# Mean and root of four RMS norms as wide tiles instead of per-token columns, in a float32 encoder trunk

## The chip, the cores and the metric

The kernel runs on one core of one Trainium2 chip. The metric is the device time of one execution, in microseconds (us). The kernel before takes 2190.19 us, the median of three runs (2189.79 to 2191.43).

## The reference

One encoder layer and a final norm, for two groups of tokens that share their weights: a prompt of 1024 tokens and a sample of 256. The change touches two of the RMS norms: `h = rmsnorm(x, norm_ffn_w)` ahead of the feed-forward block, and the last norm of the prompt.

```
def rmsnorm(x, w):
    y = x * lax.rsqrt(jnp.mean(x * x, -1, keepdims=True) + EPS)
    return y * w
...
def encoder_layer(...):
    ...                                  # token mixing, then cross-attention, each x = x + ...
    h = rmsnorm(x, norm_ffn_w)
    gu = h @ ffn_w_gate_up
    x = x + (silu(gu[..., :D_FF]) * gu[..., D_FF:]) @ ffn_w_down
    return x
...
trunk: return rmsnorm(x, final_norm_w)   # prompt and sample
```

## The kernel before, in words

Activations lie feature-major: 1024 features are eight tiles of 128 partitions (k or m = 0 to 7), and the tokens run along the free axis in three blocks: block 0 (prompt, 512 tokens), block 1 (prompt, 512) and block 2 (sample, 256). In the text they are also x0, x1 and x2, after the residual tiles that hold them.

A product in float32 accuracy is made of three products in the type float32r: each operand is split in a rounded part "hi" and a rest "lo" (`split`, L124 to L126: ScalarE copies hi, VectorE or GpSimd subtracts to get lo), and hi·hi, hi·lo and lo·hi are added up in a PSUM bank (`mm3`, L110, which calls `mm`, L108). So nearly every TensorE row of the profile is L108, and nearly every split L125 and L126.

A norm needs, for each token, a sum over 1024 features, which lie on partitions and tiles. `Norm.add` (L241) squares a tile on ScalarE (L250, L253) and adds it to `nacc`, a tile of 128 partitions by tokens (L254, on VectorE, in the last norm on GpSimd). `Norm.rest` (L257) then does:

- the sum: for each 128 tokens a true float32 product of `nacc` with a column of ones. TensorE makes each float32 product in two passes, so four of them are eight instructions. The result is one column for each 128 tokens;
- the root, on VectorE (L271 and `rsqrt`, L225): a first guess from the bits and three Newton steps, eleven instructions on 128x4 numbers;
- after a lag, the spreading of the root over all partitions: four float32 products of the root's columns (`nst`, broadcast) with the identity, eight instructions again;
- the normalisation, L289: x times weight times the spread root, which stands in a PSUM bank. In the last norm some tiles (`SHARED`) go another way: ScalarE multiplies by the weight, and GpSimd by a copy of the root (L281, L284, L285).

The order of work. TensorE's order is the program's own: the main generator issues matmuls and advances a modelled clock (`K.clock`), and side generators (the norms) are pumped when that clock passes their due time. `yield lag` in a norm thus sets after how many modelled nanoseconds its sum, and with `lag2` its spreading, is put among the main matmuls. TensorE works in that order strictly; where a matmul's input is late, all that follows waits. The other engines' orders are made by a scheduler from a cost model, and each engine also works strictly in its order.

Around the feed-forward norm: `OutProj.run` (L1451) makes the attention's output projection, first two tiles m of all blocks, then m = 2 to 7 of block 0, then of block 1, then of block 2. Each tile's evacuation (L1462) adds to x and then to the norm. After a block's last tile its x is stored to memory (`x2d`, L1492) and its norm is started as a side (L1497). The normalisation overwrites x in place, so it waits for that store. Meanwhile GpSimd and ScalarE prepare feed-forward weights (`after`, L1835: two weight splits, then four additions at L1847). Then `ff_first` (L2052) multiplies four products of the normalised blocks 0 and 1 for the first feed-forward tile: `pa` and `pu` of block 0, `pb` and `pv` of block 1, then the sample. Block 2's sum stands half way in `pa`, its spreading in `pb`. The results go through a SiLU (tanh on ScalarE, L1914). The feed-forward products are made with sums and differences of the normalised halves, which VectorE prepares from x0 and x1 (`make_r1`, L1867; `make_r2`, L1874 and L1875; `make_t34`, L1882).

At the end: `down_prompt` (L2203) finishes block 1 of the prompt and then block 0, each followed by `last_norm` (L2260) as a side, beside the last prompt products and the sample's products. Normalised tiles are stored by transfers that ScalarE's and SyncE's queues issue in turn (L2264).

Of the kernel before, what the change touches and what calls it, by code (L numbers as in the profile page):

```python
# [17 lines left out]
P = 128  # L18
D = 1024
KT = D // P  # L20
# [6 lines left out]
EPS = 1e-6  # L27
# [10 lines left out]
S_MIX, S_XA, S_MEM, S_FFN, S_FIN, S_CONV, S_DNW, S_LNW, S_LNB = 0, 8, 16, 24, 32, 40, 100, 101, 105  # L38
# [16 lines left out]
class Trunk:  # L55
# [68 lines left out]
    def split(self, hi, lo, src, eng=None):  # L124
        self.last_hi = self.nc.scalar.activation(hi, src, AF.Copy).ins  # L125
        (eng or self.nc.vector).tensor_tensor(out=lo, in0=src, in1=f32(hi), op=ALU.subtract)  # L126
# [37 lines left out]
def trunk_kernel(ctx: ExitStack, tc: tile.TileContext, a):  # L164
    nc = tc.nc
    V, S, G, T, SY = nc.vector, nc.scalar, nc.gpsimd, nc.tensor, nc.sync
    K = Trunk(ctx, tc, a)
# [19 lines left out]
    n = 0  # L187
# [44 lines left out]
    class Norm:  # L232
# [21 lines left out]
                (eng or V).tensor_tensor(out=self.acc, in0=self.acc, in1=sq, op=ALU.add)  # L254
            self.k += 1

        def rest(self, xk, wcol, sink, pace=1300, shared=(), lag=1500, ks=range(KT), inplace=False, ready=None, halves=1, lag2=2800, rooms=()):  # L257

            p, n = self.p, self.n
            nb = n // P  # L260
            yield lag
# [7 lines left out]
            y = p.tile([P, 4 if p is xp else 16], F32, tag="nst", name="nst", bufs=2)[:, :nb]  # L269
# [12 lines left out]
            for k in ks:  # L282
                if k in shared:
                    S.activation(xk(k), xk(k), AF.Copy, scale=sm[:, wcol + k : wcol + k + 1])  # L284
                    G.tensor_tensor(out=xk(k), in0=xk(k), in1=rb, op=ALU.mult)  # L285
                    sink(k, xk(k))
                    continue
                t = bank() if k in rooms else xk(k) if shared or inplace else p.tile([P, 512], F32, tag="nsq", name="nt", bufs=self.sq)[:, :n]
                V.scalar_tensor_tensor(out=t, in0=xk(k), scalar=sm[:, wcol + k : wcol + k + 1], in1=pb[:, :n], op0=ALU.mult, op1=ALU.mult)  # L289
                sink(k, t)  # L290
                yield pace * n / 512

    def rstd_of(nm, y, lag, lag2=0, halves=1):
        n = nm.n
# [109 lines left out]
    parts = []  # L404
# [7 lines left out]
    pb = bank()  # L412
# [1016 lines left out]
    class OutProj:  # L1429
# [21 lines left out]
        def run(self, xsrc, scale, wcol, xpool, store, sinks=None, then=None, after=None):  # L1451


            ps = (xpool,) * 3 if sinks is None else (x0p, xhp, xpool)
            x = [p.tile([P, KT, n], F32, tag=f"x{b}", name=f"x{b}") for b, (p, (_, n)) in enumerate(zip(ps, BLOCKS))]
            for ks in (slice(0, 2), slice(2, 8)):
                for b, (t0, n) in enumerate(BLOCKS):
                    SY.dma_start(x[b][:, ks, :], xsrc[:, ks, t0 : t0 + n])
            nms = [Norm(xpool, n) for _, n in BLOCKS]

            def evac(m, b, ps):
                V.scalar_tensor_tensor(out=x[b][:, m, :], in0=ps, scalar=scale, in1=x[b][:, m, :], op0=ALU.mult, op1=ALU.add)  # L1462
                nms[b].add(x[b][:, m, :])

            begun, self.first = self.first, []
            for i, (m, b) in enumerate((m, b) for m in range(2) for b in range(3)):
                if i < len(begun):
                    yield from proj(begun[i], self.ws[m], self.src, b, range(KT - 2, KT))
                    evac(m, b, begun[i])
                else:  # L1470
                    yield from self.parts(m, b, range(KT))
                    evac(m, b, self.first[-1])
                if (m, b) == (1, 0):
                    K.ahead()
            hs = self.hs
            for b, (t0, n) in enumerate(BLOCKS):
                for m in range(2, KT):
                    if b == 0:
                        self.ws.append(K.take())
                    ps = bank(pm)[:, :n]  # L1480
                    yield from proj(ps, self.ws[m], self.src, b)
                    if b == 0 and m < KT - 1 or b == 2 and m == 6:
                        K.ahead()
                    evac(m, b, ps)
                    if b == 2 and after is not None:
                        after(m)
                if b == 0:
                    hs += act_tiles()
                if then is not None and b == 0:
                    then()  # L1490
                if store is not None:
                    SY.dma_start(store[:, :, t0 : t0 + n], x[b])  # L1492
                xk = lambda k, b=b: x[b][:, k, :]
                if sinks is None:
                    norm_b = nms[b].rest(xk, wcol, to_h(hs, b), 600)
                else:
                    norm_b = nms[b].rest(xk, wcol, sinks(b, hs), PACES[b], ks=range(KT) if b != 1 else SECOND_KS, inplace=True, lag2=LAGS2[b])  # L1497
                K.pending[id(hs), b] = K.side(norm_b)
            self.x = x

# [759 lines left out]
    def last_norm(nm, b):  # L2260
# [3 lines left out]
            (SY if k % 2 else S).dma_start(a["yT"][:, k, t0 : t0 + n], t)  # L2264

        if b < 2:
            K.side(nm.rest(lambda k: x2[b][:, k, :], S_FIN, sink, PACEF, SHARED[b], LAGF[b], lag2=LAGF2[b]))
            return
        pb = bank()
        ms, y = pb[:, :n], pb[:, n : 2 * n]  # L2270
# [205 lines left out]
```

## Time and profile before

| | |
|---|---|
| median of three runs | 2190.19 us |
| the profiled execution, its time | 2190.45 us |
| its span, first to last instruction | 2188.7 us |
| outside the span | 1.75 us |
| TensorE (PE) busy | 2174.0 us, 99% |
| VectorE (DVE) busy | 1354.3 us, 62% |
| ScalarE (ACT) busy | 879.9 us, 40% |
| GpSimd (POOL) busy | 569.7 us, 26% |
| mean granted TensorE clock | 0.999 |

How to read the rows: a timeline row gives the start in us, the time to the end of its last instruction, engine, line, operation, output and inputs, shape, and the count of merged instructions; in brackets stands how long the engine was idle before and what ended that. Matmuls overlap, so what one costs TensorE is the distance from its start to the next start, not its length.

### The profile page before, as it was taken

To read this page: it belongs to the slowest core of one execution; us is meant where nothing else is said; L and a number is where in the kernel's file an instruction comes from. 1 tells how busy PE (TensorE), PEld (TensorE's weight loads), DVE (VectorE), ACT (ScalarE), POOL (GpSimd) and SP (SyncE) were. 2 spreads that over 40 slices of the span, in tenths; PEclk is the share of its full clock that TensorE was granted. 3 is DMA by queue.
4 is the path that set the end of the run, shared out by engine and by line. 5 is a ranking of instruction groups with operands and counts; after the bars stand their busy time and mean duration, and the time that the engine had idled before them with its cause. 6 is when DMAs were issued, how large, how long until landed. Compare 5 with 4: busy or idle time off the path is not lost.

```text
span 2188.7 us, 32379 instructions
## 1 busy us (share of the span) xinstructions
PE 2174.0 (99%) x12436; PEld 1905.0 (87%) x12436; DVE 1354.3 (62%) x2614; ACT 879.9 (40%) x1649; POOL 569.7 (26%) x379
## 2 busy tenths in 40 slices
PE   9999999999999999999999999999999999999998
PEld 8988888898888899888988888888888888888888
DVE  7867587686874855677644556644434444378575
ACT  6533262544535553224544533332322323343454
POOL 2010010100000000142412332566666665200031
PEclk9999999999999999999999999999999999999999
DMA  5221412323234546741512521222222222493631
GB/s 194 92 93 58 119 56 91 81 66 93 75 118 126 168 139 202 243 147 39 192 67 97 171 100 63 102 84 87 82 77 78 84 97 92 143 349 120 206 111 58
DMA packets 188309, 255.13 MB, mean 117 GB/s; under 512 B 71978, under 2 KB 102266, under 8 KB 188154
## 3 DMA queue, kind: packets, MB, share of 16 engines
q1 hardware_dynamic: 170618, 228.15, 31.7%
q10 hardware_dynamic: 17536, 24.91, 3.1%
q8 instruction: 97, 1.59, 0.3%
q14 instruction: 58, 0.48, 0.1%
HBM read 179.05 MB, written 73.97 MB: 116 GB/s over the span
## 4 chain that ended last, share of the span: by engine, by line
PE 92%; DVE 5%; ACT 2%; DMA 1%; issue 1%; SPq 0%; POOL 0%; DVEq 0%; ACTq 0%
PE bank L108 91%; PE bank L121 1%; DVE acc L690 1%; DVE U L932 1%; DMA braw<-gq 1%; DMA raw<-in_w_sv 0%; DVE zt L924 0%; ACT U L914 0%; ACT UT L911 0%; DVE nt L289 0%; DVE gb L811 0%; DVE gs L690 0%; ACT junk L513 0%; ACT acc L688 0%; DVE lo L126 0%
## 5 line engine op out<-in xcount | busy, mean ns | idle before, releaser
L108 PE MATMUL bank<-hi,whi 128*128 128x512 f32 (+1 forms) x1976 | 701.2, 355 | 0.2 <-DVE vg L489 0.2
L108 PE MATMUL bank<-lo,whi 128*128 128x512 f32 (+1 forms) x1976 | 686.8, 348 | 0.0
L108 PE MATMUL bank<-hi,wlo 128*128 128x512 f32 (+1 forms) x1976 | 686.8, 348 | 0.0
L108 PEld LDWEIGHTS bank<-hi,wlo 128*128 128x128 f32 x1976 | 373.6, 189 | 48.2
L108 PEld LDWEIGHTS bank<-hi,whi 128*128 128x128 f32 x1976 | 374.4, 189 | 44.4 <-DVE vg L489 1.0
L108 PEld LDWEIGHTS bank<-lo,whi 128*128 128x128 f32 x1976 | 374.5, 190 | 42.8
L125 ACT ACTIVATE whi<-raw 128x1024 fp32r<-128x1024 f32 (+1 forms) x136 | 136.9, 1009 | 248.6 <-PE bank L108 218.9
L126 POOL TENSOR_TENSOR wlo<-raw,whi 128x1024 fp32r<-128x1024 f32 x65 | 158.4, 2439 | 295.5 <-ACT whi L125 295.5
L108 PE MATMUL bank<-bhl,whi 128*128 128x512 f32 x408 | 125.9, 390 | 0.0
L126 DVE TENSOR_TENSOR wlo<-raw,whi 128x1024 fp32r<-128x1024 f32 (+1 forms) x71 | 80.7, 1139 | 70.5 <-ACT whi L125 70.3
L126 POOL TENSOR_TENSOR wlo<-x,whi 128x1024 fp32r<-128x1024 f32 x40 | 96.5, 2412 | 47.5 <-ACT whi L125 47.5
L2107 DVE TENSOR_TENSOR x<-x,bank 128x512 f32<-128x512 f32 x21 | 14.5, 689 | 125.1 <-ACT x L1902 125.1
L690 DVE SCALAR_TENSOR_TENSOR acc<-craw,sm,acc 128x510 f32<-128x510 f32 (+1 forms) x96 | 73.8, 769 | 27.6 <-ACT acc L688 25.9
L108 PEld LDWEIGHTS bank<-bhl,whi 128*128 128x128 f32 x408 | 76.4, 188 | 16.4 <-ACT whi L125 0.4
L1915 DVE SCALAR_TENSOR_TENSOR t<-t,x 128x512 f32<-128x512 f32 x42 | 63.9, 1520 | 28.4 <-ACT t L1914 28.4
L125 ACT ACTIVATE whi<-x 128x1024 fp32r<-128x1024 f32 (+1 forms) x48 | 49.2, 1025 | 77.2 <-PE bank L108 69.3
L108 PE MATMUL bank<-bhl,wlo 128*128 128x512 f32 x204 | 79.6, 390 | 0.5 <-DVE wlo L126 0.5
L108 PE MATMUL bank<-bhl,ahl 128*128 128x512 f32 x312 | 75.0, 395 | 0.0
L1924 DVE SCALAR_TENSOR_TENSOR t<-bank,t 128x512 f32<-128x512 f32 (+1 forms) x44 | 24.5, 558 | 81.4 <-PE bank L108 81.4
L1051 ACT ACTIVATE gs<-bank 128x512 f32<-128x512 f32 (+1 forms) x60 | 31.2, 519 | 103.2 <-PE bank L108 93.8
L1902 ACT ACTIVATE x<-bank 128x512 f32<-128x512 f32 x63 | 37.7, 599 | 82.8 <-PE bank L108 80.1
L108 PEld LDWEIGHTS bank<-bhl,ahl 128*128 128x128 f32 x312 | 58.7, 188 | 13.7
(416 smaller groups left out, 4513.5 us busy)
## 6 DMA issues: line engine op xcount, KB each, us to landing
raw<-in_w_gu SPq DMA_DIRECT2D x44, 512.0 KB, 3.4
braw<-gq SPq DMA_DIRECT2D x14, 1024.0 KB, 6.4
raw<-in_w_g SPq DMA_DIRECT2D x20, 512.0 KB, 3.3
gq<-t SPq DMA_DIRECT2D x33, 256.0 KB, 2.0
gtd<-gs ACTq DMA_DIRECT2D x32, 256.0 KB, 2.4
w<-in_w_dn SPq DMA_DIRECT2D x8, 1024.0 KB, 11.0
raw<-in_w_qkv SPq DMA_DIRECT2D x12, 512.0 KB, 3.5
gq<-r SPq DMA_DIRECT2D x22, 256.0 KB, 2.0
```

Of the source, the lines that this page charges most:

```text
L108: self.nc.tensor.matmul(out, l, r, start=start, stop=stop, skip_group_check=more)
L121: self.nc.tensor.transpose(out, x, ident)
L125: self.last_hi = self.nc.scalar.activation(hi, src, AF.Copy).ins
L126: (eng or self.nc.vector).tensor_tensor(out=lo, in0=src, in1=f32(hi), op=ALU.subtract)
L690: V.scalar_tensor_tensor(out=dst, in0=src, scalar=wj, in1=dst, op0=ALU.mult, op1=ALU.add)
L932: V.scalar_tensor_tensor(out=U[d][:, hs, :], in0=quad(pu), scalar=mine[:, 2 * level + d : 2 * level + d + 1], in1=U[d][:, hs, :], op0=ALU. ...
L1051: S.activation(t, ps, AF.Tanh, scale=0.5)
L1902: S.activation(t, ps, AF.Copy)
L1915: V.scalar_tensor_tensor(out=t, in0=t, scalar=1.0, in1=src, op0=ALU.add, op1=ALU.mult)
L1924: V.scalar_tensor_tensor(out=out, in0=u, scalar=sign, in1=t, op0=ALU.mult, op1=ALU.mult)
L2107: V.tensor_tensor(out=c22, in0=c22, in1=pe, op=ALU.add)
```

## The change

`rest` gets a parameter `means`; with it the norm goes through the new method `wide`. There a 128x128 stationary operand whose every element is 1/1024 is multiplied with `nacc` as the moving operand: one product over all 512 tokens gives each token's mean, already on all partitions. ScalarE takes the reciprocal root of the bank (function Abs_reciprocal_sqrt, L315 of the new code), and VectorE makes one Newton step with three instructions of 128x512 (L316 to L318) in the PSUM bank. There is no second product.

- Feed-forward norm, blocks 0 and 1: `nacc` is split into hi and lo, and there are two float32r products. They are placed 3000 ns of modelled time after the block's last tile (`LAGW`); before, the sum was at 1500, and the spreading 2800 (block 0) or 9500 (block 1) later. Block 2 keeps the old way.
- The prompt's last norm, blocks 1 and 0: no split, one float32 product, at 13500 and 15500 (before: the sum at 6000 and 8000, the spreading 9000 later).

```
+        def room(self, name, dt=F32):
+            return self.p.tile([P, 512], dt, tag="nsq", name=name, bufs=self.sq)[:, : self.n]
+
+        def wide(self, means, hilo, xk, wcol, sink, pace, shared, lag, ks, inplace):
+            n = self.n
+            parts = [self.acc] if self.apart is None else [self.acc, self.apart]
+            hls = []
+            for x in parts:
+                if hilo:
+                    hls += [self.room("nhi", F32R), self.room("nlo", F32R)]
+                    split(*hls[-2:], x, V)
+                else:
+                    hls.append(x)
+            yield lag
+            pb = bank()[:, :n]
+            for t in hls:
+                mm(pb, means, t, t is hls[0], t is hls[-1])
+            r = self.acc
+            S.activation(r, pb, AF.Abs_reciprocal_sqrt, bias=eps)
+            V.scalar_tensor_tensor(out=pb, in0=pb, scalar=EPS, in1=r, op0=ALU.add, op1=ALU.mult)
+            V.scalar_tensor_tensor(out=pb, in0=pb, scalar=-0.5, in1=r, op0=ALU.mult, op1=ALU.mult)
+            V.scalar_tensor_tensor(out=pb, in0=pb, scalar=1.5, in1=r, op0=ALU.add, op1=ALU.mult)
+            if shared:
+                S.activation(self.acc, pb, AF.Copy)
...
-                    norm_b = nms[b].rest(xk, wcol, sinks(b, hs), PACES[b], ks=range(KT) if b != 1 else SECOND_KS, inplace=True, lag2=LAGS2[b])
+                    norm_b = nms[b].rest(xk, wcol, sinks(b, hs), PACES[b], lag=LAGW[b], ks=range(KT) if b != 1 else SECOND_KS, inplace=True, lag2=9500, means=means if b < 2 else None)
...
-            K.side(nm.rest(lambda k: x2[b][:, k, :], S_FIN, sink, PACEF, SHARED[b], LAGF[b], lag2=LAGF2[b]))
+            K.side(nm.rest(lambda k: x2[b][:, k, :], S_FIN, sink, PACEF, SHARED[b], LAGF[b], means=mean.to_broadcast([P, P]), hilo=False))
...
-FIRST_W, PACES, LAGS2 = 9000, (600, 1300, 600), (2800, 9500, 9500)
+FIRST_W, PACES, LAGW = 9000, (600, 1300, 600), (3000, 3000, 1500)
-LAG0, LAGF, LAGF2, PACEF = 9700, (8000, 6000, 1500), (9000, 9000, 2800), 1000
+LAG0, LAGF, PACEF = 9700, (15500, 13500), 1000
```

The change also moves instructions on VectorE and ScalarE. New line numbers are 41 to 45 above the old: L328 is the normalisation (before L289), L1507 the evacuation (L1462), L1912, L1919, L1920 and L1927 the preparations (L1867, L1874, L1875, L1882), L1959 the tanh (L1914).

First place: VectorE at the end of the output projection. x1 is being normalised and split (lo1, and wlo for its first half), x2's last tiles are evacuated, squared and added; the last addition to `nacc_12579` is what TensorE's sum for block 2 reads. Before:

```order
L254 TENSOR_TENSOR nacc_12579<-nacc_12579,nsq_13268 128x256
L289 SCALAR_TENSOR_TENSOR x1_12569<-x1_12569,sm_78,bank_13286 128x512 x2
L1462 SCALAR_TENSOR_TENSOR x2_12570<-bank_13273,x2_12570 128x256
L126 TENSOR_TENSOR lo1_12883<-x1_12569,hi1_12882 128x512 x2
L254 TENSOR_TENSOR nacc_12579<-nacc_12579,nsq_13307 128x256
L289 SCALAR_TENSOR_TENSOR x1_12569<-x1_12569,sm_78,bank_13286 128x512 x2
L1462 SCALAR_TENSOR_TENSOR x2_12570<-bank_13312,x2_12570 128x256
L126 TENSOR_TENSOR lo1_12883<-x1_12569,hi1_12882 128x512 x2
L254 TENSOR_TENSOR nacc_12579<-nacc_12579,nsq_13344 128x256
```

The same engine with the change, its last rows up to the same addition (now of `nsq_13339`):

```order
L254 TENSOR_TENSOR nacc_12579<-nacc_12579,nsq_13268 128x256
L328 SCALAR_TENSOR_TENSOR x1_12569<-x1_12569,sm_78,bank_13162 128x512
L1507 SCALAR_TENSOR_TENSOR x2_12570<-bank_13273,x2_12570 128x256
L328 SCALAR_TENSOR_TENSOR x1_12569<-x1_12569,sm_78,bank_13162 128x512
L126 TENSOR_TENSOR wlo_13235<-x1_12569,whi_13234 128x512
L254 TENSOR_TENSOR nacc_12579<-nacc_12579,nsq_13302 128x256
L126 TENSOR_TENSOR wlo_13272<-x1_12569,whi_13271 128x512
L328 SCALAR_TENSOR_TENSOR x1_12569<-x1_12569,sm_78,bank_13162 128x512
L1507 SCALAR_TENSOR_TENSOR x2_12570<-bank_13307,x2_12570 128x256
L1912 TENSOR_TENSOR x0_12568<-x0_12568,x1_12569 128x1024
L126 TENSOR_TENSOR wlo_13272<-x1_12569,whi_13271 128x512
L254 TENSOR_TENSOR nacc_12579<-nacc_12579,nsq_13339 128x256
```

Before, four of x1's eight normalisations and four splits stood ahead of that addition. Now all eight stand ahead of it (the first five above these rows), with eight splits (four lo1 and the first of four wlo stand above these rows) and one L1912. Counted from x1's first normalisation they are, with four evacuations and four additions for x2 (this addition among them), 25 instructions.

Second place: VectorE in `ff_first` around the last steps of block 2's root, the last L230 of `nst`, which TensorE's spreading for block 2 reads (`nst_13372` before, `nst_13364` with the change). The small steps of the root (L228 to L230, 128x2) stand between preparations of x0 and x1. Before:

```order
L126 TENSOR_TENSOR wlo_13272<-x1_12569,whi_13271 128x512
L229 TENSOR_TENSOR bank_13369<-bank_13369,nst_13372 128x2
L289 SCALAR_TENSOR_TENSOR x1_12569<-x1_12569,sm_78,bank_13286 128x512
L230 SCALAR_TENSOR_TENSOR nst_13372<-bank_13369,nst_13372 128x2
L1867 TENSOR_TENSOR x0_12568<-x0_12568,x1_12569 128x1024
L228 SCALAR_TENSOR_TENSOR bank_13369<-nst_13372,bank_13369 128x2
L126 TENSOR_TENSOR wlo_13272<-x1_12569,whi_13271 128x512
L229 TENSOR_TENSOR bank_13369<-bank_13369,nst_13372 128x2
L1867 TENSOR_TENSOR x0_12568<-x0_12568,x1_12569 128x1024
L230 SCALAR_TENSOR_TENSOR nst_13372<-bank_13369,nst_13372 128x2
L1924 SCALAR_TENSOR_TENSOR t_13402<-bank_13351,t_13402 128x512
```

With the change:

```order
L228 SCALAR_TENSOR_TENSOR bank_13361<-nst_13364,bank_13361 128x2
L1919 TENSOR_TENSOR x1_12569<-x1_12569 128x1024
L229 TENSOR_TENSOR bank_13361<-bank_13361,nst_13364 128x2
L1920 SCALAR_TENSOR_TENSOR x1_12569<-x1_12569,x0_12568 128x1024
L230 SCALAR_TENSOR_TENSOR nst_13364<-bank_13361,nst_13364 128x2
L1969 SCALAR_TENSOR_TENSOR t_13388<-bank_13346,t_13388 128x512
L228 SCALAR_TENSOR_TENSOR bank_13361<-nst_13364,bank_13361 128x2
L126 TENSOR_TENSOR wlo_13306<-x1_12569,whi_13305 128x1024
L229 TENSOR_TENSOR bank_13361<-bank_13361,nst_13364 128x2
L126 TENSOR_TENSOR wlo_13343<-x1_12569,whi_13342 128x1024
L230 SCALAR_TENSOR_TENSOR nst_13364<-bank_13361,nst_13364 128x2
L1927 SCALAR_TENSOR_TENSOR x0_12568<-x1_12569,x0_12568 128x1024
```

Before, the root's last step stood ahead of the instruction that takes `pu`'s bank (L1924), and before it two 128x512 splits and two L1867. Now it stands behind that instruction (L1969), with two 128x1024 splits (wlo) between. The follower of the first tanh (L1915, now L1960) stands two rows above the first rows shown before, and three above those shown now.

Third place: ScalarE at the first tanh, with the engines that each row waits for. Before:

```order
L125 ACTIVATE whi_13240<-x1_12569 128x512 [waits DVE_49,PE_49,Pool_49]
L125 ACTIVATE whi_13240<-x1_12569 128x512 [waits DVE_49]
L1914 ACTIVATE t_13402<-bank_13350 128x512 [waits PE_49,Activation_49]
L125 ACTIVATE whi_13271<-x1_12569 128x512 [waits DVE_49,Pool_49]
L125 ACTIVATE whi_13271<-x1_12569 128x512 [waits DVE_49]
```

With the change:

```order
L125 ACTIVATE whi_13271<-x1_12569 128x512 [waits DVE_49]
L253 ACTIVATE nsq_13339<-x2_12570 128x256 [waits DVE_49,Activation_49]
L125 ACTIVATE hi1_12884<-x0_12568 128x1024 [waits DVE_49] x2
L1959 ACT_TABLE_LOAD [waits PE_49]
L1959 ACTIVATE t_13388<-bank_13345 128x512 [waits Activation_49]
```

The reciprocal root needs another function table than tanh, so a table load now stands ahead of the first tanh, and it is the load that waits for TensorE's `pa`. Another load stands ahead of block 0's L315, without a wait, and a third ahead of the last norm's first L315; the one that the sample's last norm had (L2367) is gone.

More of the change, by code (lines that the diff above doesn't have):

```diff
@@ L255, in add, with rest @@
             self.k += 1
-        def rest(self, xk, wcol, sink, pace=1300, shared=(), lag=1500, ks=range(KT), inplace=False, ready=None, halves=1, lag2=2800, rooms=()):
+        def rest(self, xk, wcol, sink, pace=1300, shared=(), lag=1500, ks=range(KT), inplace=False, ready=None, halves=1, lag2=2800, rooms=(), means=None, hilo=True):
             p, n = self.p, self.n
             nb = n // P
+            if means is not None:
+                yield from self.wide(means, hilo, xk, wcol, sink, pace, shared, lag, ks, inplace)
+                return
             yield lag
@@ L268, in rest @@
                     mm(pc[:, c : c + 1], t[:, c * P : (c + 1) * P], one, t is parts[0], t is parts[-1])
-            y = p.tile([P, 4 if p is xp else 16], F32, tag="nst", name="nst", bufs=2)[:, :nb]
+            y = p.tile([P, 4 if p is xp else 16], F32, tag="nst", name="nst", bufs=2 if p is xp else 1)[:, :nb]
             ms, sc = pc[:, 4 : 4 + nb], pc[:, 8 : 8 + nb]
@@ L291, in rest, with means_of @@
                 yield pace * n / 512
+        def room(self, name, dt=F32):
[21 more added lines that the diff above has]
+                S.activation(self.acc, pb, AF.Copy)
+            for k in ks:
+                if k in shared:
+                    S.activation(xk(k), xk(k), AF.Copy, scale=sm[:, wcol + k : wcol + k + 1])
+                    G.tensor_tensor(out=xk(k), in0=xk(k), in1=self.acc, op=ALU.mult)
+                    sink(k, xk(k))
+                    continue
+                t = xk(k) if shared or inplace else self.room("nt")
+                V.scalar_tensor_tensor(out=t, in0=xk(k), scalar=sm[:, wcol + k : wcol + k + 1], in1=pb, op0=ALU.mult, op1=ALU.mult)
+                sink(k, t)
+                yield pace * n / 512
+    def means_of(p, n):
+        t = p.tile([P, n], F32R, tag="mean", name="mean")[:, :1]
+        V.tensor_copy(t, mean)
+        return t.to_broadcast([P, P])
     def rstd_of(nm, y, lag, lag2=0, halves=1):
@@ L1459, in run @@
             nms = [Norm(xpool, n) for _, n in BLOCKS]
+            means = None if sinks is None else means_of(xpool, 16)
             def evac(m, b, ps):
```

## The prediction

> **What bounds the kernel now.** I read the page's busy times first, then the shares of the chain that ended last, then TensorE's waits.
>
> ```profile
> PE 2174.0 (99%) x12436; PEld 1905.0 (87%) x12436; DVE 1354.3 (62%) x2614; ACT 879.9 (40%) x1649; POOL 569.7 (26%) x379
> PE 92%; DVE 5%; ACT 2%; DMA 1%; issue 1%; SPq 0%; POOL 0%; DVEq 0%; ACTq 0%
> PE bank L108 <- DVE vg L489: 1.2, 2, 1.0
> ...
> PE bank L108 <- DVE nacc L254: 0.2, 1, 0.2
> ```
>
> TensorE is busy for 2174.0 us and is 92% of the chain. The third number of a wait row is its total, the last the longest single wait: none is above 1.0 us, and the norm sums made TensorE wait 0.2 us once. So there is no slack on TensorE. What a change takes out of its order shortens the run by its full length, and what it adds, work or wait, lengthens it. VectorE and ScalarE count only where TensorE waits for them, and their order around the norms is where that can begin. TensorE's timeline has the prices:
>
> ```profile
> 0.95 5.49 PE L389 MATMUL bank<-shared 128*128 128x512 f32 x6 [0.95 <-POOL shared L383]
> 6.23 3.08 PE L108 MATMUL bank<-first,shared 128*128 128x256 f32 x12
> 9.15 2.75 PE L389 MATMUL bank<-shared 128*128 128x512 f32 x6
> ...
> 1296.93 0.39 PE L108 MATMUL bank<-hi,wlo 128*128 128x512 f32 x1
> 1297.16 0.95 PE L108 MATMUL bank<-cst,nacc 128*128 128x1 f32 x8
> 1297.97 0.49 PE L108 MATMUL bank<-hi,whi 128*128 128x512 f32 x1
> 1298.29 0.40 PE L108 MATMUL bank<-lo,whi 128*128 128x512 f32 x1
> ...
> 1301.51 1.05 PE L108 MATMUL bank<-cst,nst 128*128 128x128 f32 x8
> 1302.32 0.48 PE L108 MATMUL bank<-hi,whi 128*128 128x512 f32 x1
> 1302.64 0.39 PE L108 MATMUL bank<-lo,whi 128*128 128x512 f32 x1
> ...
> 1351.10 0.50 PE L108 MATMUL bank<-cst,nacc 128*128 128x1 f32 x4
> ...
> 1361.75 0.61 PE L108 MATMUL bank<-cst,nst 128*128 128x128 f32 x4
> ```
>
> Only distances between starts count. A usual 128x512 product takes 0.23 (1296.93 to 1297.16). A group of eight small float32 instructions and the product behind it take 1.13, for the sum (1297.16 to 1298.29) as for the spreading (1301.51 to 1302.64). Less that product's 0.23, a group costs 0.90.
>
> **A: TensorE's own work, -4.7.** Four norms lose two groups each: 8 x 0.90 = 7.2, and the 0.2 wait above, which is block 1's sum (it starts 0.24 late at 1331.35), goes with them: 7.4. Added are four float32r products of 128x512 in the feed-forward norm, 4 x 0.23 = 0.9, and two float32 products of 128x512 at the end. The row at 9.15 holds three such products (six passes) in 2.75, so 0.9 each, 1.8 in all. Net -7.4 + 2.7 = -4.7 (-4.9 to -4.4, the second if each of the four places keeps the 0.1 that a product behind a change of operands takes beyond 0.23). Of this, 2.9 lies ahead of block 2's sum: 4 x 0.90 + 0.2 - 0.9. Without any wait TensorE thus reaches that sum at 1351.10 - 2.9 = 1348.2 (times here are of the profile before, shifted by what was saved).
>
> **B: a new wait at block 2's sum, +4.8.** The sum reads the last addition to `nacc` on VectorE, and the first place of the order shows what now stands ahead of it. I need when x1's normalisation can start and how long VectorE then takes.
>
> ```profile
> 1334.59 2.43 DVE L254 TENSOR_TENSOR nacc<-nacc,nsq 128x256 f32<-128x256 f32 x1 [0.23 <-ACT nsq L253]
> ...
> 1344.23 1.41 DVE L289 SCALAR_TENSOR_TENSOR x<-x,sm,bank 128x512 f32<-128x512 f32 x2
> ...
> 1350.73 0.75 DVE L289 SCALAR_TENSOR_TENSOR x<-x,sm,bank 128x512 f32<-128x512 f32 x1
> ...
> 1357.23 1.22 DVE L1867 TENSOR_TENSOR x<-x,x 128x1024 f32<-128x1024 f32 x1
> ```
>
> ```profile
> 1334.33 2.41 POOL L126 TENSOR_TENSOR wlo<-raw,whi 128x1024 fp32r<-128x1024 f32 x1 [21.64 <-ACT whi L125]
> 1337.21 2.41 POOL L126 TENSOR_TENSOR wlo<-raw,whi 128x1024 fp32r<-128x1024 f32 x1 [0.47 <-ACT whi L125]
> 1339.70 5.59 POOL L1847 TENSOR_TENSOR raw<-raw 128x512 f32<-128x512 f32 x4
> ```
>
> ```profile
> 1329.88 0.51 SPq L1492 DMA_DIRECT2D x2d<-x  x1
> ```
>
> ```profile
> x2d<-x SPq DMA_DIRECT2D x2, 2048.0 KB, 8.4
> ```
>
> The start: the normalisation overwrites x1, so it waits for the store of x1. That was issued at 1329.88 and is now 1.35 earlier (block 0's two groups against two products), 1328.5; with the median landing of 8.4 for the two stores, 1336.9. Before, the normalisation began at 1344.23, since block 1's spreading stood there; that hold is what the change removes. The other bound is an L254 of x2 ahead of it: at 1334.59 such an addition took 2.43 beside GpSimd's 2.41, and one caught by the second split would end near 1337.9. I take 1337.4.
>
> The length: from 1344.23 to 1350.73 VectorE made exactly the mix of the rows shown in the order before: four normalisations, four splits, two evacuations, two additions, in 6.5 us. The new order needs twice that, 13.0, and one 128x1024 addition, 1.2 (the row at 1357.23): 14.2. That stretch lay almost wholly behind GpSimd's four additions (1339.70 to 1345.29); now they run beside it, and the 2.43 above shows that an addition can be drawn out. For this I add 1.4, with ends 0 and 2.0, nearer to the upper, since 5.6 us of the stretch are covered. So the addition ends at 1337.4 + 14.2 + 1.4 = 1353.0, TensorE waits 1353.0 - 1348.2 = 4.8. Lowest 1336.9 + 14.2 = 1351.1, a wait of 2.9; highest 1337.9 + 14.2 + 2.0 = 1354.1, 5.9. Behind the waiting sum stands the rest of `pa` and all that follows, so it counts in full.
>
> **C: a second wait, at block 2's spreading, +2.0.** TensorE reaches it 1361.75 - 1351.10 = 10.65 after the sum, if nothing else waits. ScalarE's timeline gives the chain to the root, with the issues of its queue near the end:
>
> ```profile
> 1354.53 0.60 ACT L1914 ACTIVATE t<-bank 128x512 f32<-128x512 f32 x1 [1.41 <-PE bank L108]
> ...
> 2138.85 0.82 ACTq L2264 DMA_DIRECT2D yT<-x  x2
> ...
> 2149.04 1.28 ACT L2367 ACT_TABLE_LOAD   x1
> 2150.33 0.30 ACT L2367 ACTIVATE shared<-nacc,shared 128x1 f32<-128x1 f32 x1
> ```
>
> The tanh, released by `pa`, started 1354.53 - 1351.10 = 3.4 after the sum. Now a table load stands there: 1.3 (2149.04 to 2150.33), then tanh 0.6: 5.3 after the sum. In the second place of the order VectorE then has two 128x512 steps (L1960, L1969; 0.65 each from the 1.41 for two) and five of 128x1024 (three L1919/L1920, two wlo; 1.2 each), 7.3 with the overlap of neighbours spent on the small root steps. The root is ready 12.6 after the sum, 2.0 late. Before, its last step came ahead of L1924 and TensorE did not wait. If the overlap is larger it is 1.0, if GpSimd or a late `pu` slows a step 2.5. As the chain starts at `pa`, this wait stands whether or not B comes.
>
> On the load the two sources differ. The Trainium skill ("ScalarE: Activation LUTs", section "What ACT_TABLE_LOAD costs") gives 1283 ns and a drain of 1380 ns for every switch of set; in the row at 2149.04 only the first is seen, with the next activation 0.01 us behind it. By the page C would be an estimated 3.4.
>
> **D: stores at the end, +0.2.** Block 0's shared tiles are finished on GpSimd by steps of 128x512, some 1.4 us each (5.59 for four such at 1339.70); their stores on ScalarE's queue now stand in a row, so that weight splits wait behind an issue that waits for GpSimd: up to 2 x 1.4 + 0.4 (half of 0.82) = 3.2. A stall that long, of the two issues at 2138.85, is already there without a wait of TensorE, so only what exceeds it counts: 0 to 0.6, and I take 0.2.
>
> **At nothing:** the last norm's three 128x512 steps instead of eleven small ones and its table load run beside sample products, which need neither; were the load in the way of a weight split, 1.3 less the buffered work. The single `nst` buffer, the copy of the mean and the order on SyncE come where VectorE idles or nobody waits. Block 1's split of `nacc` has 3 us of modelled lag for two steps of about 0.65; without that cover it would cost up to 1.3.
>
> **Sum:** -4.7 + 4.8 + 2.0 + 0.2 = +2.3. Against the profiled execution's own 2190.45 this is 2192.75; the median is 0.26 lower, so I forecast **2192.5**. The ends of the terms give 2189 (-4.9 + 2.9 + 1.0) to 2194.8 (-4.4 + 5.9 + 2.5 + 0.6).
>
> **The rivals.** *VectorE keeps up.* If x1's normalisation starts as soon as its root is there and nothing slows it, B vanishes: 2190.2 - 4.7 + 2.2 = 2187.7; if the preparations run ahead too, so that C goes, 2185.7. For it: before, the store was not what held x1. Against: 14.2 us of steps in 1348.2 - 1336.9 = 11.3. Chance 0.18, of which 0.07 for both.
>
> *The clock falls (slower).* The first six passes of the run took 5.49, the same six at 9.15 took 2.75: after its idle start TensorE ran at half rate. If the stop at B is long enough, the same comes once more. Price: the start lost 2.7 on the first six passes; but the chain of C begins at `pa`, which the slow stretch delays too, so part of C is covered: net about 2.2, and 2194.7. It decides if a stop of between 1.0 (the longest single wait in the first view) and 4.8 is enough; no row here settles that. Chance 0.22. The Trainium skill ("TensorE: Matmul & The Clock Gate", Part 1) says half clock is the default state and comes back after an idle window of about 3.4 us; by that rule a stop of 4.8 can suffice, and one of 2.9 not.
>
> *The change does not do what it says, or the load is dear.* If the wide products cost a change of operand as a group does (0.9 instead of 0.23), A shrinks to -2.0 and the time is 2195.2; with the skill's drain instead, 2193.9. Against: the 0.95 of a group is made of eight instructions. Chance 0.10.
>
> **How the numbers follow.** My case has 0.50. A measurement of this kernel can tell about 0.2%, 4.4 us, from no change: under 2185.8 or over 2194.6. Faster: most of the 0.07 with neither wait, and a little of my case: 0.08. Slower: some 0.14 of the clock case, 0.05 of the third, 0.03 of my own upper end: 0.22. The rest, 0.70, is the same. The range for 8 in 10 reaches from 2187.0, below which lies the best half of the first rival, to 2195.6, past the clock's price with the upper part of B.
>
> **What would show it.** Right: on TensorE a wait of 3 to 6 us for `nacc` at block 2's sum and one of 1 to 2.5 for `nst` at its spreading; x1's first normalisation released by the store; a table load ahead of the first tanh; eight groups of eight gone and six wide products in their place. Wrong: no such waits (then 2188 or less), a granted clock below 1 behind the stop, or wide products that hold TensorE longer than 0.3 (0.9 at the end). If TensorE waits elsewhere, at blocks 0 and 1's own sums or in the sample's products, I have missed a place.

## The result: slower by half a per cent

| | before | after |
|---|---|---|
| median | 2190.86 us (6 runs) | 2201.91 us (6 runs) |
| ratio, 95% interval | | 1.0052, 1.0041 to 1.0062 |
| profiled execution, its time | 2190.45 us | 2201.36 us |
| its span | 2188.7 us | 2199.6 us |
| mean granted TensorE clock | 0.999 | 0.997 |

The change costs 11 us where I had forecast a time within the noise, 2192.5, with 2195.6 as the top of my range. The page of after has the busy times and the chain:

```profile
PE 2174.9 (99%) x12380; PEld 1902.4 (86%) x12380; DVE 1356.4 (62%) x2585; ACT 886.6 (40%) x1657; POOL 566.0 (26%) x379
PE 89%; DVE 6%; issue 2%; ACT 2%; POOL 1%; DMA 0%; SPq 0%; DVEq 0%; ACTq 0%; POOLq 0%
```

TensorE has 56 instructions less, is as long busy as before (2174.0), and waits more: its share of the chain fell from 92% to 89%. TensorE's waits, and its timeline around `ff_first`, show where:

```profile
PE bank L108 <- DVE nacc L254: 6.2, 1, 6.2
PE bank L108 <- DVE nst L230: 2.7, 2, 2.1
```

```profile
1347.80 0.39 PE L108 MATMUL bank<-hi,wlo 128*128 128x512 f32 x1
1354.38 1.02 PE L108 MATMUL bank<-cst,nacc 128*128 128x1 f32 x4 [6.19 <-DVE nacc L254]
1355.26 0.78 PE L108 MATMUL bank<-hi,whi 128*128 128x512 f32 x1
1355.84 0.63 PE L108 MATMUL bank<-lo,whi 128*128 128x512 f32 x1
1356.26 0.63 PE L108 MATMUL bank<-hi,wlo 128*128 128x512 f32 x1
...
1367.54 0.39 PE L108 MATMUL bank<-hi,wlo 128*128 128x512 f32 x1
1369.99 1.03 PE L108 MATMUL bank<-cst,nst 128*128 128x128 f32 x4 [2.07 <-DVE nst L230]
1370.67 0.77 PE L108 MATMUL bank<-hi,whi 128*128 128x512 f32 x1
```

Two things are to be seen. Both stops stand where the prediction put them, 6.19 us at block 2's sum and 2.07 at its spreading. And behind each stop the products are longer, 0.63 instead of 0.39, and their starts lie 0.42 apart instead of 0.23. The table of windows of the same kernel says why (columns: the stretch, its length, TensorE's busy time and instructions, granted clock, DMA share, GB/s):

```profile
1349.80:1353.20 3.40, 0.00 (x0) 0.99 0.00 0
1353.20:1356.60 3.40, 2.22 (x7) 0.50 0.87 308
1356.60:1360.00 3.40, 3.40 (x9) 0.50 0.00 0
1360.00:1363.40 3.40, 3.40 (x16) 1.00 0.00 0
...
1366.80:1370.20 3.40, 1.33 (x6) 1.00 0.20 77
1370.20:1373.60 3.40, 3.40 (x11) 0.50 0.00 0
1373.60:1377.00 3.40, 3.40 (x16) 0.99 0.00 0
```

The granted clock is halved for 6.8 us at the first stop, from 1.2 us before its end on, and for 3.4 us behind the second. Subtracting the starts of the same instruction in the two timelines gives the whole account:

| instruction | before | after | later by | what lies between |
|---|---|---|---|---|
| product in the output projection | 1344.15 | 1341.09 | -3.06 | saved work |
| first product at full clock again, in `pa` | 1354.05 | 1360.06 | 6.01 | stop 6.19, half clock 2.88 |
| last product ahead of the spreading | 1361.53 | 1367.54 | 6.01 | |
| first at full clock behind it | 1364.27 | 1374.21 | 9.94 | stop 2.07, half clock 1.86 |
| product in the last feed-forward tiles | 1880.27 | 1890.22 | 9.95 | |
| product in `down_prompt` | 2070.05 | 2080.86 | 10.81 | 0.5 of it a wait for a split, the rest not followed up |
| last norm of the sample | 2179.33 | 2190.23 | 10.90 | saved work 1.9, given back |

A stop is counted here from the end of the last product, 0.16 us after the place where the next one was due (0.39 against 0.23). Counted from there the stops are 6.35 and 2.23, and the half clock costs 2.7 and 1.7.

At the end nothing is gained, though block 1's and block 0's last norms lost their groups of eight. VectorE there before:

```profile
2101.81 2.73 DVE L289 SCALAR_TENSOR_TENSOR x<-x,sm,bank 128x512 f32<-128x512 f32 x4 [2.71 <-ACT nacc L281]
...
2109.65 0.68 DVE L2225 SCALAR_TENSOR_TENSOR x<-bank,x 128x512 f32<-128x512 f32 x1
```

VectorE, GpSimd and TensorE there with the change:

```profile
2114.40 2.73 DVE L328 SCALAR_TENSOR_TENSOR x<-x,sm,bank 128x512 f32<-128x512 f32 x4 [0.23 <-ACT nacc L320]
2117.04 3.44 DVE L126 TENSOR_TENSOR gs<-graw,gs 128x512 fp32r<-128x512 f32 x2
...
2121.01 1.27 DVE L2270 SCALAR_TENSOR_TENSOR x<-bank,x 128x512 f32<-128x512 f32 x2
```

```profile
2114.45 5.49 POOL L324 TENSOR_TENSOR x<-x,nacc 128x512 f32<-128x512 f32 x4 [16.44 <-ACT nacc L320]
```

```profile
2125.00 0.51 PE L108 MATMUL bank<-gs,whi 128*128 128x256 f32 x2 [0.84 <-DVE x L2270]
```

TensorE is some 10 us behind in this place. Block 1's normalisation (L328) starts 12.6 us later than before, so 2.6 later against TensorE's work. Two splits beside GpSimd take 3.44, and the evacuations of block 0's last tiles (L2270, 11.4 later) are late for the sample's products, which need their banks: a wait of 0.84, and short delays of the products behind it. By the starts of the same products, the wait and these delays add up to 1.9.

### The profile page after: what moved, and what is told of

Same layout as the page of the kernel before. It is cut to its first block, busy times and chain, and to the rows that moved or that the text cites. A ratio compares the mean times of both kernels' runs of the same rounds, so it can differ in the third digit from the quotient of the medians.

```text
span 2199.6 us, 32236 instructions
## 1 busy us (share of the span) xinstructions
PE 2174.9 (99%) x12380; PEld 1902.4 (86%) x12380; DVE 1356.4 (62%) x2585; ACT 886.6 (40%) x1657; POOL 566.0 (26%) x379
## 4 chain that ended last, share of the span: by engine, by line
PE 89%; DVE 6%; issue 2%; ACT 2%; POOL 1%; DMA 0%; SPq 0%; DVEq 0%; ACTq 0%; POOLq 0%
PE bank L108 88%; PE bank L121 1%; DVE acc L734 1%; DVE U L976 1%; DVE lo L126 0%; DVE nacc L254 0%; DMA raw<-in_w_sv 0%; DVE wlo L126 0%; DVE zt L968 0%; ACT U L958 0%; POOL x L324 0%; DVE x L328 0%; ACT UT L955 0%; ACT whi L125 0%; DVE nt L292 0%
## 5 line engine op out<-in xcount | busy, mean ns | idle before, releaser
L1960 DVE SCALAR_TENSOR_TENSOR t<-t,x 128x512 f32<-128x512 f32 x42 | 63.7, 1516 | 29.1 <-ACT t L1959 29.1
L1969 DVE SCALAR_TENSOR_TENSOR t<-bank,t 128x512 f32<-128x512 f32 (+1 forms) x44 | 24.5, 558 | 81.4 <-PE bank L108 81.4
```

Of the source, the lines that this page charges most:

```text
L1960: V.scalar_tensor_tensor(out=t, in0=t, scalar=1.0, in1=src, op0=ALU.add, op1=ALU.mult)
L1969: V.scalar_tensor_tensor(out=out, in0=u, scalar=sign, in1=t, op0=ALU.mult, op1=ALU.mult)
```

## The experiments

My theory after this comparison: the order on VectorE makes the stops, the stops make the half clock, and at the end the place of block 1's product makes the late evacuation. The rivals: the clock falls for another reason; the wide norm itself costs; VectorE has no time to spare there, so that any order stops TensorE somewhere. All ratios are to the kernel before, run on the same chip with each group of runs; its median was between 2190.24 and 2191.37. So a difference of some 1 us between medians of two groups shows nothing by itself, and the traces have to tell.

| run | median us | ratio, 95% interval |
|---|---|---|
| feed-forward part alone | 2199.36 | 1.0041, 1.0029 to 1.0054 |
| first stop filled | 2199.32 | 1.0038, 1.0024 to 1.0052 |
| both filled | 2198.22 | 1.0033, 1.0021 to 1.0045 |
| block 1 at 12300 | 2194.21 | 1.0016, 1.0007 to 1.0025 |
| end alone | 2192.82 | 1.0009, 1.0000 to 1.0018 |
| end alone, at 10500 | 2191.08 | 1.0003, 0.9994 to 1.0012 |
| without GpSimd's additions | 2197.98 | 1.0032, 1.0020 to 1.0045 |
| feed-forward alone, block 1 at 9500 | 2190.00 | 0.9998, 0.9989 to 1.0006 |
| block 2's sum at 8000 | 2197.47 | 1.0028, 1.0018 to 1.0038 |
| both parts placed, sum at 2700 | 2187.93 | 0.9986, 0.9977 to 0.9995 |
| both parts placed, sum at 1500 | 2187.31 | 0.9986, 0.9978 to 0.9995 |
| end alone, at 10500, old addresses | 2188.97 | 0.9988, 0.9979 to 0.9997 |

### Is it the stop that halves the clock?

```
             pc = bank()
+            if fill is not None:
+                for _ in range(27):
+                    nc.tensor.matmul(pc, fill[:, 0:P], fill, start=True, stop=True)
```

> The changed kernel, with 27 products of 128x512 (about 6.1 us) put ahead of block 2's sum into the bank that the sum then overwrites; nothing is left out. Theory (the stop itself brings the half clock): TensorE never stops there, the slow stretch behind it goes, and the time falls by its 2.9 us although work was added: 2199.0 us; the second slow stretch stays if each stop has its own. Rival 1 (the clock falls for another reason than the stop): no change, 2201.9 us. Rival 2 (the second slow stretch is the tail of the first): 2197.1 us.

Measured 2199.32, as the theory had it: 27 more products, and 2.6 us less time (2.0 if each is taken against its own before). The windows, by which the stretch from the filled sum on is at full clock:

```profile
1348.00:1356.00 8.00, 7.92 (x38) 1.00 0.32 115
1356.00:1364.90 8.90, 8.90 (x41) 1.00 0.04 14
1365.00:1368.40 3.40, 0.45 (x3) 1.00 0.20 77
1368.40:1371.80 3.40, 2.83 (x9) 0.52 0.03 5
```

The second slow stretch stays, so it is not the tail of the first. Its stop even grew to 3.52 us. TensorE came to the spreading 2.5 us earlier, but the root was ready only 1.0 earlier, because the scheduler's order now had two more 128x1024 steps of VectorE (1.2 each) ahead of the root's last step. Nine more products ahead of the spreading:

> The same with 9 more products (2.0 us) ahead of block 2's spreading. Theory: both slow stretches go, 2.9 + 1.9 us: 2197.1 us, and the granted clock is 1.00 throughout. Rival (a stop of 2 us is too short to matter, the slow rows behind it have another cause): 2199.0 us, as with the first filling alone.

2198.22 was measured, 1.1 above the theory: the nine were too few for the longer stop, and 1.48 us of it were left. The clock did what was expected of it; the second of these windows holds the short stop, the third is behind it:

```profile
1365.00:1368.40 3.40, 3.40 (x16) 1.00 0.04 16
1368.40:1371.80 3.40, 1.92 (x11) 1.00 0.18 66
1371.80:1375.00 3.20, 3.20 (x15) 1.00 0.00 0
```

So each of the two stops of the changed kernel brought its half clock, and one of 1.5 us did not.

### What makes the first stop 6.2 us long?

```
             for x, y in (...):
-                G.tensor_tensor(out=x, in0=x, in1=y, op=ALU.add)
+                pass
```

> The changed kernel without GpSimd's four additions at the end of the output projection; sums of two weights that the later products read are thereby left out, so only the time is of use. Theory (what made the stop 6.2 us and not about 3.5 is that VectorE's splits are drawn out beside these additions, 4.6 us for three instead of 1.9): the stop shrinks to 3.5 us and the time by 2.7 us if the clock still falls, 2199.2 us, or by 5.6 us if it does not, 2196.3 us. Rival (the splits wait for something else): no change, 2201.9 us.

The stop came out at 3.5 us, and the time at 2197.98, 1.2 below the theory's number for a clock that still falls, as it did at both stops. VectorE's rows of after, GpSimd's of after, and VectorE's of this run:

```profile
1337.64 2.06 DVE L328 SCALAR_TENSOR_TENSOR x<-x,sm,bank 128x512 f32<-128x512 f32 x3
1339.61 4.58 DVE L126 TENSOR_TENSOR lo<-x,hi 128x512 fp32r<-128x512 f32 x3
```

```profile
1337.51 6.13 POOL L1892 TENSOR_TENSOR raw<-raw 128x512 f32<-128x512 f32 x4
```

```profile
1339.65 1.89 DVE L126 TENSOR_TENSOR lo<-x,hi 128x512 fp32r<-128x512 f32 x3
```

The same three splits (lo), started at the same time, take 4.58 beside GpSimd and 1.89 without it: 2.7 us, the whole difference of the stops. The Trainium skill ("SBUF — State Buffer", section "Who interferes with whom") has the rule: VectorE and GpSimd share one pair of ports as an exclusive lock, and a VectorE instruction with two inputs in SBUF contends with a GpSimd instruction that reads SBUF. These rows agree, 1.53 for each split as for each addition; the normalisations, whose second input is a PSUM bank, were not drawn out (2.06 for three at 1337.64, beside the same additions).

### Can the order be mended?

First by moving block 1's products behind block 2's additions:

```
-FIRST_W, PACES, LAGW = 9000, (600, 1300, 600), (3000, 3000, 1500)
+FIRST_W, PACES, LAGW = 9000, (600, 1300, 600), (3000, 12300, 1500)
```

> The changed kernel with block 1's two wide products placed at 12300 of modelled time instead of 3000, so that six of x1's eight normalisations stand behind x2's last addition on VectorE, and the table load ahead of the first tanh waits for nothing. Theory: no stop at block 2's sum, none or a short one at its spreading, full clock: 2190.9 - 3.0 (feed-forward's part of the saving) = 2187.9 us, up to 2188.8 with the 0.9 us that the changed kernel loses between the feed-forward's start and the end. Rival (the wide norm itself, its products, its VectorE steps or the table loads, is what costs): 2195 us or more.

2194.21: the theory's number was missed by 6 us. Both stops were gone but for 0.8 us, and TensorE was 1.8 us ahead of before at 1389. Then its timeline has this, and VectorE's shows what came late:

```profile
1389.09 0.40 PE L108 MATMUL bank<-wlo,whi 128*128 128x512 f32 x1
1391.89 0.80 PE L108 MATMUL bank<-whi,wlo 128*128 128x512 f32 x1 [2.40 <-DVE wlo L126]
```

```profile
1378.18 4.21 DVE L1927 SCALAR_TENSOR_TENSOR x<-x,x 128x1024 f32<-128x1024 f32 x2
...
1388.39 2.85 DVE L1960 SCALAR_TENSOR_TENSOR t<-t,x 128x512 f32<-128x512 f32 x1
1391.16 2.36 DVE L126 TENSOR_TENSOR wlo<-raw,whi 128x512 fp32r<-128x512 f32 x2
```

What TensorE waited for is the first of the two splits at 1391.16. VectorE had no idle time from 1375 on, so what was put later pushed everything behind it, and two steps were drawn out beside GpSimd: 4.21 for the pair L1927 (2.35 before) and 2.85 for L1960 (0.68 before). The stop of 2.40 halved the clock again, and by 1400 TensorE was 3.7 us behind. Here the rival that VectorE has no slack was right.

Then by moving the consumer, block 2's sum. Its spreading, whose lag is counted from the sum, moves with it by the same 30 products:

```
-FIRST_W, PACES, LAGW = 9000, (600, 1300, 600), (3000, 3000, 1500)
+FIRST_W, PACES, LAGW = 9000, (600, 1300, 600), (3000, 3000, 8000)
```

> The changed kernel with one number changed: block 2's sum at 8000 of modelled time instead of 1500, so that TensorE makes 30 more products of pa (6.8 us) before it; VectorE's order up to x2's last addition is the same. Theory (VectorE was late only for the place at which TensorE asked): TensorE asks about 0.7 us after the addition is ready, neither stop is left or only some tenths at the spreading, the clock stays full: 2201.9 - 6.2 - 2.9 - 2.1 - 1.9 = 2188.8 us. Rival (the stretch is short of VectorE time, so the wait only moves to the products of the next tile): 2193 us or more.

2197.47, a miss again. The stop at the sum was gone, and a stop of 3.78 us stood at the spreading, with half clock behind it:

```profile
1369.41 1.22 PE L108 MATMUL bank<-cst,nst 128*128 128x128 f32 x4 [3.78 <-DVE nst L230]
```

TensorE made the sum at about the same time as in the changed kernel (1354.76 against 1354.38) and came to the spreading 10.9 us later. ScalarE's tanh and VectorE's last step of the root:

```profile
1355.74 0.60 ACT L1959 ACTIVATE t<-bank 128x512 f32<-128x512 f32 x1
```

```profile
1369.20 0.15 DVE L230 SCALAR_TENSOR_TENSOR nst<-bank,nst 128x2 f32<-128x2 f32 x1
```

The tanh was 6.1 us earlier than in the changed kernel (1361.82), so it did not hold the root. VectorE had no idle time from the sum until that step, 14.6 us: the scheduler's order now had two L1927 (1.2 each) ahead of it, which stand behind it in the changed kernel. So the rival was right too, only that the wait moved to the spreading. Last, about the place where block 1's spreading had stood before (15 small products ahead of it):

```
-LAGW = (3000, 3000, 1500), LAGF = (15500, 13500)
+LAGW = (3000, 9500, 1500), the last norm as before
```

> The feed-forward norm with block 1's products at 9500 (where its spreading stood before), the last norm as before. VectorE then has four of x1's normalisations and four splits ahead of x2's last addition, as before, and the table load ahead of the first tanh waits for TensorE. Theory (order, not work): a wait of at most 0.6 us at the sum and about 1 us at the spreading, too short for the clock; 2190.2 - 3.0 + 1.6 = 2188.8 us. Rival (VectorE has no slack in this stretch, so whatever is put later there comes back as a stop further on, as the one of 2.4 us with block 1 at 12300): 2192 us or more.

2190.00, not to be told from before, 1.2 above the theory's number and well under the rival's. The order did what the theory wanted, with a stop of 1.1 us at the sum, none added at the spreading and the clock full. By the timelines this execution lost 0.7 us ahead of the feed-forward norm, where nothing was changed, and won 1.7 in it.

### The two parts apart, and the end

> The feed-forward norm as in the changed kernel, the last norm as before. Theory (all of the loss is made at block 2's sum and spreading; at the end the 1.9 us that TensorE saves are given back by the late evacuation of block 0): 2201.9 us, within 0.7 of the changed kernel. Rival (the end does save its 1.9 us, and something else costs more in the middle): 2203.8 us.

2199.36, 2.5 below the changed kernel and outside what I expected (the two intervals overlap, so the traces have to tell). By the account of starts this kernel is 7.6 us behind at 2070 and 7.6 at the end, the changed one 10.81 and 10.90; so the changed end gives nothing, and the difference of 3.3 was made earlier: 0.4 at the first slow stretch, 1.6 at the second, and 1.2 between 1890 and 1950, which I did not follow up. The second slow stretch is missing: with almost the same stop, 2.04 us up to 1369.57, the windows read

```profile
1365.90:1369.30 3.40, 1.63 (x8) 1.00 0.20 77
1369.30:1372.70 3.40, 3.13 (x16) 1.00 0.00 0
```

The slow stretch of the first stop began 0.9 us earlier here (1352.3 against 1353.2), so a grid of 3.4 us lies differently over the second stop: one of its lines, at 1369.3, falls 0.2 before the stop's end; see below.

> The feed-forward norm as before, the prompt's last norm as in the changed kernel. Theory (TensorE saves 1.9 us of work, and loses about as much because block 1's normalisation runs later on VectorE, beside GpSimd, and holds up the evacuation of block 0): within 1 us of before, 2189.5 to 2191.2, with a wait of 0.8 us for the evacuation. Rival (the end gains by itself): 2188.4 us and no such wait.

> The same with block 1's product at 10500 of modelled time instead of 13500, about 3 us earlier, which is where the spreading's normalisation began before. Theory: the wait for the evacuation goes and the 1.9 us stay: 2188.4 us. Rival (the wait has another cause, such as ScalarE's copy of the root or the table load): as the end alone at 13500.

The edit is `LAGF = (15500, 10500)` instead of `(15500, 13500)`. Medians 2192.82 and 2191.08: their difference, 1.7, is what the theory gave to the early place, but both are some 2 us too high. The traces show the end itself as expected: with 13500 the wait of 0.8 us for the evacuation and no gain from 2030 to the end; with 10500 no such wait, and TensorE 4.95 us behind at 2070 but 3.12 at the end, 1.8 won. (Of the 4.95, 2.0 come from the first 60 us of this execution, the slowest of its eleven; the clock was halved there for 3.4 us.) What was too high in both lay in the feed-forward, where nothing was to have changed. TensorE with the end alone:

```profile
1473.23 0.40 PE L108 MATMUL bank<-t4h,whi 128*128 128x512 f32 x1
1473.47 0.40 PE L108 MATMUL bank<-t4l,whi 128*128 128x512 f32 x1
1473.70 0.40 PE L108 MATMUL bank<-t4h,wlo 128*128 128x512 f32 x1
```

Before, the same products start 0.227 apart (1472.21 to 1472.89 for three), here 0.233, in stretches that add up to 1.9 us later starts between 1420 and 1890. I had taken the tile `mean` out of the feed-forward norm and left `nst` with one buffer, so that all tiles behind them lay 64 bytes lower. One number puts that back:

```
-            y = p.tile([P, 4 if p is xp else 16], F32, tag="nst", name="nst", bufs=2 if p is xp else 1)[:, :nb]
+            y = p.tile([P, 4 if p is xp else 16], F32, tag="nst", name="nst", bufs=2)[:, :nb]
```

> The last norm alone, block 1's product at 10500, with one number more changed: the small tile nst has two buffers again, as before the change, which moves all tiles that stand behind it in that pool by 64 bytes. The orders of all engines are those of the run with the end early. Theory (in the two runs of the end alone the feed-forward's products stood 0.233 us apart instead of 0.227 in places, 1.9 us in all, because the tile mean was left out there and nst had one buffer, so that the weights lay 64 bytes lower): the 1.9 us go and the end's own 1.8 us show: 2188.9 us. Rival (those longer products come by chance of the execution): 2191 us as before.

2188.97, the theory's number. So the end's part alone, placed at 10500, is faster than before (0.9988, 0.9979 to 0.9997), and the shifted addresses had hidden it.

### Both parts placed

> Both norms wide, with block 1's feed-forward products at 9500, block 2's sum at 2700 and block 1's last product at 10500. Theory: the two parts add up, the feed-forward's 3.0 us and the end's 1.9 us: 2186.3 us, up to 2187.5 if some tenths of wait stay. Rival (the parts don't add up, because one stop is traded for the next): 2189.5 us or more, not to be told from before.

> The same with block 2's sum left at 1500. Theory: the stop of 1.1 us at that sum stays, too short for the clock, so 1.2 us above the run with the sum at 2700: 2187.5 us. Rival (the sum's place does not matter): no difference between the two.

2187.93 and 2187.31. The first is 0.4 above the theory's upper end. Both beat before by 0.14%, and the two cannot be told apart, which is the rival's forecast for the second: with the sum at 2700 its stop is gone, but a wait for a split of 1.3 us stands behind it, with the sum at 1500 the stop of 1.1 stands as in the run at 9500:

```profile
PE bank L108 <- DVE nacc L254: 1.1, 1, 1.1
```

## Why the prediction was wrong

**The step that failed** is that the sum has no term for the clock: it takes TensorE to run at full clock behind its stops. I had the slower clock as the second rival, with a chance of 0.22 and a net price of 2.2 us for one fall. The clock fell twice, and the two falls cost 2.88 and 1.86, 4.7 us together; what I took off because the chain of C would cover part of the price was not there, for that chain begins at the end of `pa` and slid with it (the stop at the spreading was 2.07 all the same). I had also written that one fall needs a long stop, and looked only at B: C, priced at 2.0, sufficed.

**A** held on TensorE: -3.06 ahead of the sum against -2.9, and about -1.9 at the end against -1.8.

**B** had the right place and mechanism, 6.19 instead of 4.8, above its upper end of 5.9. The start was right in time (1337.64 against 1337.4), but by the other bound than the store. The store, issued at 1328.48, landed within 7.4 us; VectorE came to the normalisation straight from an addition for x2 that was drawn out beside GpSimd:

```profile
1336.57 1.15 DVE L254 TENSOR_TENSOR nacc<-nacc,nsq 128x256 f32<-128x256 f32 x1
```

So the sign that I had named, a normalisation released by the store, did not come, and the place between the two bounds was luck. The length was wrong: I gave 1.4 for GpSimd's additions, at most 2.0, and the run without them shows 2.7. My own row, the addition drawn out to 2.43, was the sign; three splits in a row each met an addition.

**C** was 2.07 against 2.0, by the chain that I had given. Whether it stands without B, as I had said, these runs do not show: with the first stop filled, or the sum moved, VectorE's order had changed too, and the wait was 3.52 and 3.78. The load behaved as in the row that I had used: ScalarE's timeline of after has no gap behind it, so the drain that the Trainium skill ("ScalarE: Activation LUTs", section "What ACT_TABLE_LOAD costs") adds did not show here either:

```profile
1360.53 1.28 ACT L1959 ACT_TABLE_LOAD   x1 [3.97 <-PE bank L108]
1361.82 0.60 ACT L1959 ACTIVATE t<-bank 128x512 f32<-128x512 f32 x1
```

**D** was 0: ScalarE's splits were held for 3.5 us, and TensorE did not wait for them.

**At nothing** was the end, and that was wrong: the last norm's steps run beside sample products, but VectorE also evacuates the banks that those products need next. A normalisation that came 2.6 us later in TensorE's time cost the 1.9 us that the products had saved; placed 3 us earlier it cost nothing.

Predicted -4.7 + 4.8 + 2.0 + 0.2 = +2.3; measured in the same terms -5.0 + 6.2 + 2.1 + 0, and beside them 4.7 for the clock, 1.9 at the end and 0.9 between, 10.8 of the 10.9 us of the spans.

## What to carry to other kernels

Where one engine is busy all the time, a stop of 2 us can cost nearly twice its length, as 2.07 with 1.86 of half clock did here: price the slower clock behind each stop with the stop itself, and count every stop. Moving work on an engine without slack trades one wait for the next, so look past the first wait, at the next tile and at the banks that the engine must empty; the places that worked here were about those where the old version's last step had stood. And when a part is taken out for an experiment, keep the addresses of what lies behind it.

## What the runs showed of the hardware

**The clock is decided on a grid of 3.4 us.** In one execution the changes of the granted clock lie whole multiples of about 3.41 us apart: in after at 1353.2, 1360.0, 1370.2 and 1373.6, without GpSimd's additions at 1351.3, 1358.1, 1368.4 and 1371.8. Each slow stretch at these stops lasted 3.4 or 6.8 us, and it began at the grid's next line, not with the stop. The Trainium skill ("TensorE: Matmul & The Clock Gate", Part 1) describes such a free-running window of about 3.4 us; its rule that the clock falls after one idle window is too mild by these runs, since windows that were idle for 2.07 (after), 1.93 (without GpSimd's additions) and 1.6 us (block 1 at 12300) were followed by half clock; the last two of them, from the windows without GpSimd's additions and with block 1 at 12300, each with the window behind it:

```profile
1365.00:1368.40 3.40, 1.47 (x9) 1.00 0.20 77
1368.40:1371.80 3.40, 3.40 (x9) 0.50 0.00 0
```

```profile
1387.60:1391.00 3.40, 1.77 (x7) 1.00 0.04 13
1391.00:1394.40 3.40, 2.51 (x6) 0.52 0.43 141
```

The window with 1.48 us (both filled) was not, nor was the one with 1.8 us in the run of the feed-forward part alone, though 1.6 sufficed elsewhere. So idle time alone does not decide. The run of both parts with the sum at 1500 shows it more plainly: near its start stands a window in which the profile has TensorE idle for 0.2 us only, but at work on 16 small float32 products of 128x1 among others, and half clock followed:

```profile
24.80:28.20 3.40, 3.21 (x22) 1.00 0.34 119
28.20:31.60 3.40, 3.40 (x17) 0.50 0.54 192
```

The same products did not bring it in the kernel before, where the clock is at 1.00 there. What is counted, and where the bound is, stays open.

**64 bytes of address** changed the distance of many products from 0.227 to 0.233 us and with it the time by 1.9 us; putting them back undid it. It was not the number of `nst` buffers: the changed kernel has one too, but keeps `mean`, and its products lag by the same 9.9 us from 1374 to 1890. Which operand it was is open.
